# Last x tiles of the output product, step order of the second norm, and three first splits in one decoder layer

## The chip, the cores and the metric

The program runs on one core of one Trainium2 chip. The metric is the device time of one execution in microseconds (us), the median of the runs. The engines are TensorE (PE, matmuls, with its weight loads PEld), VectorE (DVE), ScalarE (ACT), GpSimd (POOL) and SyncE (SP), which here issues most DMAs. Each engine works through its own instructions in their order and waits on semaphores for the others.

## What is computed

One decoder layer on x (2048 rows, width 1024), all in 32-bit floats:

```
h    = RMSNorm(x) * (1 + scale1) + shift1
p    = h @ W_in            -> q, k, v (8 heads of 64), forget logits, x_in, B, C (512 each)
attn = causal softmax(q.k/8 + F[t] - F[s]) v,   F = cumsum(log sigmoid(...)), q and k normed by head
conv = B * dwconv3(C * x_in)
x1   = x + gate1 * (concat(attn, conv) @ W_out)
h2   = RMSNorm(x1) * (1 + scale2) + shift2
u    = dwconv3(h2 @ W_up)             (2 x 2816 columns)
out  = x1 + gate2 * ((silu(u_gate) * u_val) @ W_down)
```

## The kernel before

A 32-bit product is made as three matmuls on split operands (`mm3`, L142): high by high, high by low, low by high. ACT makes the high part of a tile, and DVE then the low part as the difference, so each new operand costs one step on ACT and, behind it, one on DVE. What is wrapped in `K(...)` keeps its place in the program's order on its engine; the rest is placed by the scheduler that builds the program, by its own estimate.

**Columns of W_in.** `project` (L484) makes k and then q: it first loads and splits its eight slices of weights (`w_slice` L167, high L178, low L179), then goes through 16 tiles of 128 rows; after a tile's matmuls come the steps of the norm by head (square on ACT, sums and a Newton root on 8 columns on DVE, L517 to L521). Then the loop at L652 makes x, c and b, column group by column group, from slices that it loads and splits at its start. DVE also works on other things in that stretch, such as `mo` (L546, L548), the modulation vector's products.

**Attention, and the start of the output product.** Attention runs in steps of one block of 128 queries of two heads. A block's `nb` (L895) and two exponentials (L898) on ACT follow the maxima on DVE (L881); PE transposes the first nine 128-column blocks (`near`, L918, copied by L920 and L925), a transposing DMA the others (`far`, L911); then come the products with the values (L954 to L956) and the division (L962). Step 64 is behind the last scores; what it still runs is the end of steps 62 and 63. There the generator `mixed` is started.

**The output product.** `mixed` (L788) goes through 64 units n: quarter Q of the rows (4 tiles of 128), half hf of the columns (512), and i, one of the eight parts of the inner length. `prepare` (L775) makes a unit's operands: for Q = 0 the pair `wp` of the weights, and for hf = 0 the pair `mp` of the mixed tile `src` (L771 high, L772 low), written into the buffer that held a weight tile `wo`. It runs up to three units ahead. Unit i = 6 has no matmuls, unit i = 7 has those of both, 24; every other unit has 12 (three for each of the four row tiles), of 128x128 by 128x512. At i = 2 of hf = 0 the four x tiles of the quarter are loaded (L801), for Q = 1 into wide tiles, else into four `raw` tiles of 128x1024, of which there are four in all (`raw_tile`, L710). At i = 7 DVE adds x (L812), which also frees the accumulators for the next half, and for hf = 1 the sums are stored through POOL's queue (L814).

**The second norm, beside it.** From unit 17 on, one step of `norm2` runs after each unit: for a quarter the squares (L1093), the root and the scaling (L1100), and then by column blocks. `columns` transposes a block on PE (L1068) and copies it with scale and shift on ACT (L1070); one accumulator buffer serves all these transposes. `operand` splits a block (L1058 high, L1059 low). An even Q has two blocks (b11, b21) by k; an odd Q has b1 and b2 by k and forms the sums of a seven-product scheme: t1, t2, t3, t4 (`diff` L1061, `last_operands` L1073), in five steps per k, each splitting as it goes.

**The up weights.** `up_weights(i)` (L1142) loads two raw tiles (L1146), scales them on ACT (L1152) and forms seven pairs. The first pair has tiles of its own; from i = 1 on they are `raw` tiles. In `up` the first product of an i is copied on ACT (`p1`, L1271) before the same accumulator is used on (L1226). The weights of i + 1 are begun ahead of that copy in the program's order.

## Time and profile before

| | |
|---|---|
| median of 3 runs | 2475.0 us (2469.92 to 2476.56) |
| the profiled execution | 2468.95 us, its span 2467.1 us |
| PE busy | 2364.3 us (96%) |
| DVE, ACT, POOL busy | 1790.0, 1256.6, 358.6 us |
| DMA | 368.70 MB, mean 149 GB/s |

The stages in the span: first norm and v up to 160 us, k and q to about 357, x, c, b to 632, attention to 970, output product to 1165, then up and down for the first half of the rows to 1825 and for the second to the end. In a timeline a row is the start, the length, engine, line and operation, `out<-in`, partitions and shape, the number of like instructions in a row, and in brackets the idle time just ahead of the row and what ended it. The clock is the share of TensorE's full speed that was granted.

### The profile page before, as it was taken

The page shows a single profiled execution, that of the slowest core. Times are in us where ns is not written, and L with a number is a line of the kernel's source. Part 1 is how long each engine was busy: PE and PEld are TensorE (multiplying, and loading weights), DVE is VectorE, ACT ScalarE, POOL GpSimd, SP SyncE. Part 2 cuts the span into 40 slices and gives each one's busy share as a digit, 9 for nine tenths or more (in the row PEclk, how much of TensorE's full clock was granted, in tenths as well). Part 3 has the DMA queues.
Part 4 walks back from the last instruction along what each step waited for, and adds up shares of the span by engine and source line. Part 5 has one row for each costly group of instructions (what it writes and reads, how often), then busy time and mean ns, then how long its engine had stood idle before and what let it go on. Part 6 is the DMA issues. An engine that isn't in the chain of part 4 may idle for free.

```text
span 2467.1 us, 38327 instructions
## 1 busy us (share of the span) xinstructions
PE 2364.3 (96%) x14419; PEld 1585.8 (64%) x14419; DVE 1790.0 (73%) x3333; ACT 1256.6 (51%) x2016; POOL 358.6 (15%) x298
## 2 busy tenths in 40 slices
PE   4999999999899888998999999999999999999999
PEld 4988788888677666444444444688764444448887
DVE  7566784452799887456788888767778888885554
ACT  3533443221588887333556556555455655554333
POOL 4210111011577785000000000000000000000000
PEclk9999999999999999999999999999999999999999
DMA  8334686443598987523322222677652222226775
GB/s 240 147 118 128 169 234 194 147 147 95 119 187 178 204 170 156 181 103 127 95 86 86 87 84 77 197 225 244 205 162 86 86 90 82 94 88 219 229 228 184
DMA packets 428066, 368.70 MB, mean 149 GB/s; under 512 B 184080, under 2 KB 327784, under 8 KB 426856
## 3 DMA queue, kind: packets, MB, share of 16 engines
q1 hardware_dynamic: 420824, 349.40, 50.3%
q10 hardware_dynamic: 4752, 8.46, 1.0%
q0 software_dynamic: 2304, 8.39, 0.9%
q8 instruction: 113, 1.85, 0.3%
q14 instruction: 73, 0.60, 0.1%
HBM read 267.54 MB, written 65.08 MB: 135 GB/s over the span
## 4 chain that ended last, share of the span: by engine, by line
PE 77%; DVE 7%; DMA 6%; issue 5%; ACT 3%; POOL 1%; SPq 1%; ACTq 0%; DVEq 0%; POOLq 0%
PE acc L1226 32%; PE acc L142 24%; PE pr L142 10%; PE pv L142 3%; DMA far<-wide 3%; PE pt L918 1%; PE ps L857 1%; PE ps L858 1%; DVE near L925 1%; PE po L954 1%; DVE s_t L881 1%; DMA wx<-in_w_up_dram 1%; PE po L956 1%; PE po L955 1%; ACT s_t L898 1%
## 5 line engine op out<-in xcount | busy, mean ns | idle before, releaser
L1226 PEld LDWEIGHTS <-pair 128*128 128x128 f16 x3696 | 362.0, 98 | 443.2 <-issue 8.4
L1226 PE MATMUL acc<-t,pair 128*128 128x512 f16 x2112 | 477.4, 379 | 0.0
L1226 PE MATMUL acc<-b,pair 128*128 128x512 f16 x1584 | 364.9, 380 | 5.9 <-ACT t L1271 5.9
L1198 DVE TENSOR_TENSOR lo<-raw,hi 128x1024 fp32r<-128x1024 f32 x176 | 211.7, 1223 | 141.9 <-ACT hi L1197 141.1
L142 PE MATMUL acc<-hi 128*128 128x512 f32 x704 | 276.9, 393 | 3.4 <-DVE t L1049 3.4
L142 PE MATMUL acc<-lo,hi 128*128 128x512 f32 x704 | 274.3, 390 | 0.3 <-DVE lo L1198 0.3
L142 PE MATMUL acc<-hi,lo 128*128 128x512 f32 x704 | 274.2, 389 | 0.0
L1197 ACT ACTIVATE hi<-raw 128x1024 fp32r<-128x1024 f32 x176 | 181.8, 1054 | 163.8 <-PE acc L142 131.1
L1239 DVE SCALAR_TENSOR_TENSOR w<-w,fcw,w 128x1024 f32<-128x1024 f32 x176 | 226.1, 1285 | 34.6 <-ACT w L1234 25.3
L142 PE MATMUL acc<-wp,mp 128*128 128x512 f16 x768 | 172.2, 383 | 6.9 <-DVE raw L812 4.1
L1130 ACT ACTIVATE pair<-raw 128x1024 f16<-128x1024 f32 x132 | 138.2, 1049 | 69.1 <-DVE raw L1127 69.1
L898 ACT ACTIVATE s_t<-s_t,nb,cst 128x2048 f32<-128x2048 f32 (+15 forms) x128 | 164.7, 1288 | 5.2 <-ACT nb L895 0.4
L1234 ACT ACTIVATE w<-w,fcw 128x1024 f32<-128x1024 f32 x88 | 100.7, 1144 | 130.6 <-DVE w L1126 130.6
L1133 DVE TENSOR_TENSOR pair<-raw,pair 128x1024 f16<-128x1024 f32 x132 | 160.8, 1219 | 6.8 <-ACT pair L1130 6.8
L592 ACT ACTIVATE wx<-wx 128x512 f32<-128x512 f32 x88 | 55.6, 632 | 202.5 <-DMA wx<-in_w_up_dram 167.6
L142 PEld LDWEIGHTS acc<-hi 128*128 128x128 f32 x704 | 132.1, 188 | 34.1 <-DVE t L1049 5.5
L142 PE MATMUL pr<-hh,wh 128*128 128x512 f32 x384 | 153.4, 399 | 0.2 <-ACT wh L178 0.2
L142 PE MATMUL pr<-hh,wl 128*128 128x512 f32 x384 | 150.9, 393 | 1.1 <-DVE wl L179 1.1
L142 PE MATMUL pr<-hl,wh 128*128 128x512 f32 x384 | 151.0, 393 | 0.0
L142 PEld LDWEIGHTS acc<-hi,lo 128*128 128x128 f32 x704 | 132.2, 188 | 27.7
L142 PEld LDWEIGHTS acc<-lo,hi 128*128 128x128 f32 x704 | 132.2, 188 | 27.4 <-DVE lo L1198 0.7
L910 POOL TENSOR_TENSOR wide<-s_t,wide 128x1024 f16<-128x1024 f32 x64 | 136.8, 2138 | 5.3
(296 smaller groups left out, 4714.6 us busy)
## 6 DMA issues: line engine op xcount, KB each, us to landing
raw<-in_w_up_dram SPq DMA_DIRECT2D x88, 512.0 KB, 3.7
raw<-y_sc SPq DMA_DIRECT2D x176, 256.0 KB, 3.7
raw<-in_w_down_dram SPq DMA_DIRECT2D x176, 256.0 KB, 4.1
wx<-in_w_up_dram SPq DMA_DIRECT2D x88, 256.0 KB, 2.9
y_sc<-w SPq DMA_DIRECT2D x44, 512.0 KB, 2.6
wm<-in_w_ada_dram SPq DMA_DIRECT2D x128, 128.0 KB, 3.0
wr<-in_w_in_dram SPq DMA_DIRECT2D x40, 256.0 KB, 3.5
x_t<-in_x_dram SPq DMA_DIRECT2D x16, 512.0 KB, 5.3
```

The lines of the kernel that those rows point to most:

```text
L142: ins = T.matmul(acc, lhsT=a, rhs=b, start=st, stop=sp)
L592: K(A.activation(t, t, AF.Abs, accum_out=l1[:, n : n + 1]))
L857: K(T.matmul(ps[:, 0:cw], lhsT=qt, rhs=kh[:, c0 : c0 + cw], start=True, stop=False))
L898: K(A.activation(cols, cols, AF.Exp, bias=nb[:, p : p + 1], scale=qk[:, 4:5], accum_out=un["l"][:, p : p + 1]))
L910: K(G.tensor_tensor(wide[:, 1, :], s_t[:, WB * P : WU], wide[:, 0, :], op=ALU.subtract))
L1130: K(A.activation(hi, raw, AF.Copy))
L1133: K(V.tensor_tensor(lo, raw, hi, op=ALU.subtract))
L1197: K(A.activation(hi, raw, AF.Copy))
L1198: K(V.tensor_tensor(lo, raw, hi.bitcast(F32), op=ALU.subtract))
L1226: K(T.matmul(acc, lhsT=a, rhs=b, start=st, stop=sp, skip_group_check=True))
L1234: K(A.activation(y, u[:, 0:1024], AF.Copy, scale=fcw[:, ct : ct + 1]))
L1239: K(V.scalar_tensor_tensor(y, u[:, m : m + 1024], fcw[:, m * 44 + ct : m * 44 + ct + 1], y, op0=ALU.mult, op1=ALU.add))
```

## The change

- `project` gets its slices and calls `following()` behind the matmuls of its last tile: k emits q's slices there, q emits x's first ones, ahead of the last tile's norm steps.
- `mixed` prepares unit 0 when it is started, and it is started before the work of step 64 is emitted. From unit 14 on it prepares five units ahead.
- The x of the last quarter is loaded by halves into 128x512 tiles that use the `src` buffers, 8 loads and 8 stores of half the size in place of 4 and 4.
- `norm2` for an odd Q takes four steps per k, in an order written for two engines, with two differences for t4 in place of three, and its last low part goes into the next step. The chain starts its second part after one empty step in place of four, and no step is taken behind a unit with i = 7.

```
+        def columns_of(col):
+            return [w_slice(w_in[k * P : (k + 1) * P, col : col + AW], [P, AW]) for k in range(KD)]
+        def project(w, col, gain, dst_hi, dst_lo, hooks, lull, following):
...
+                if i == NT - 1:
+                    after = following()
...
+        last_k, w_q = project(columns_of(AW), AW, ..., lambda: columns_of(0))
+        last_q, w_x = project(w_q, 0, ..., lambda: conv_slices(0, "x", 3 * AW + H))
...
+                w[name] = conv_slices(j, name, col) if j or name != "x" else w_x
...
     def mixed():
         todo = [(Q, hf, i) for Q in range(4) for hf in range(2) for i in range(8)]
-        ready = 0
+        prepare(*todo[0])
+        ready = 1
+        yield
         for n, (Q, hf, i) in enumerate(todo):
-            while ready < min(n + 3, 64):
+            while ready < min(n + (3 if n < 14 else 5), 64):
...
+            if Q == 3 and i == 2:
+                kept[3] = [fb.tile([P, 512], F32, tag=f"src{4 * hf + t}", name="x_q") for t in range(4)]
+                for xp, r in zip(kept[3], rows):
+                    K(nc.sync.dma_start(xp, x[r, n0 : n0 + 512]))
...
-                    if hf:
+                    if Q == 3:
+                        G.dma_start(x1_sc[Q * 4 + t][:, n0 : n0 + 512], xp)
+                    elif hf:
                         G.dma_start(x1_sc[Q * 4 + t], kept[Q][t])
...
+            if s == H * nu:
+                mix = mixed()
+                next(mix)
             n = 0
             while run or n < 3:
...
                 load_mixed(0, 7)
-                mix = mixed()
...
-        def last_operands(Q, k):
-            b21, t2 = bt["b21", k], bt["t2", k]
-            t4 = temp()
-            diff(t4, b21[0], t2[0])
-            diff(t4, t4, t2[1])
-            K(V.tensor_tensor(t4, t4, b21[1], op=ALU.add))
-            operand("t4", k, t4)
...
                 b1 = columns(Q, k)
+                if k:
+                    low(t4, *t4s)
                 yield
-                b2, t3 = columns(Q, 4 + k), temp()
-                operand("b22", k, b2)
+                b2, t3, t4 = columns(Q, 4 + k), temp(), temp()
+                b22, t1s, t2s, t3s, t4s = [pair(name, k) for name in ("b22", "t1", "t2", "t3", "t4")]
+                b11, b21 = bt["b11", k], bt["b21", k]
+                high(b2, b22[0])
                 diff(t3, b2, b1)
+                diff(b1, b1, b11[0])
+                low(b2, *b22)
                 yield
-                for e in bt["b11", k]:
-                    diff(b1, b1, e)
-                operand("t1", k, b1)
+                diff(b1, b1, b11[1])
+                high(b1, t1s[0])
+                high(t3, t3s[0])
+                diff(b2, b2, b1)
+                low(b1, *t1s)
+                low(t3, *t3s)
+                high(b2, t2s[0])
                 yield
-                diff(b2, b2, b1)
-                operand("t2", k, b2)
-                operand("t3", k, t3)
+                diff(t4, b21[1], b2)
+                low(b2, *t2s)
+                K(V.tensor_tensor(t4, t4, b21[0], op=ALU.add))
+                high(t4, t4s[0])
                 yield
-                last_operands(Q, k)
+            if Q % 2:
+                low(t4, *t4s)
                 yield
...
-        early = chain(steps[0], (None for _ in range(4)), steps[1], weights)
+        early = chain(steps[0], (None for _ in range(1)), steps[1], weights)
         for n, _ in enumerate(mix, 8):
-            if n >= 17:
+            if n >= 17 and n % 8 != 7:
                 next(early, None)
```

Line numbers move with it: the pairs of `prepare` are made at L778 and L779, x is added at L826, `high` and `low` are L1074 and L1077, `diff` is L1084, the copy of `columns` L1093, the up weights' load and scaling L1170 and L1176, the copy `p1` L1295. Three places show what moves.

ACT at step 64, before: `nb` and the exponentials (L898) of step 63, the copies L920 and L971 of the blocks' transposes, and the first pairs of the output product.

```order
L895 ACTIVATE nb<-mx,cst 128x2
L898 ACTIVATE s_t,l<-s_t,nb,cst 128x1152
L898 ACTIVATE s_t,l<-s_t,nb,cst 128x1024
L920 ACTIVATE near<-pt 128x512
L971 ACTIVATE tm<-pt,vi 128x512
L920 ACTIVATE near<-pt 128x512
L920 ACTIVATE near<-pt 128x128
L771 ACTIVATE wp<-wo,rim 128x512
L771 ACTIVATE mp<-src,rim 128x512
```

And now:

```order
L778 ACTIVATE wp<-wo,rim 128x512
L778 ACTIVATE mp<-src,rim 128x512
L911 ACTIVATE nb<-mx,cst 128x2
L914 ACTIVATE s_t,l<-s_t,nb,cst 128x1152
L914 ACTIVATE s_t,l<-s_t,nb,cst 128x1024
L936 ACTIVATE near<-pt 128x512
L987 ACTIVATE tm<-pt,vi 128x512
L936 ACTIVATE near<-pt 128x512
L936 ACTIVATE near<-pt 128x128
```

The first pair moved from the end of the row to its head.

DVE around unit 39, the end of the third quarter's first half, before: the last two scalings of the norm, a mixed tile's low part, the low part of b22, t3, and then the four sums that free the accumulators.

```order
L1100 TENSOR_SCALAR w_13811<-w_13811,ss 128x1024
L1100 TENSOR_SCALAR w_13812<-w_13812,ss 128x1024
L772 SCALAR_TENSOR_TENSOR mp<-src,rim,mp 128x512
L1059 TENSOR_TENSOR b_14288<-t_14285,b_14288 128x512
L1061 TENSOR_TENSOR t_14287<-t_14285,t_14278 128x512
L812 SCALAR_TENSOR_TENSOR raw<-acc,rim,raw 128x512 x4
L1061 TENSOR_TENSOR t_14278<-t_14278,b_13911 128x512 x2
```

And now:

```order
L1115 TENSOR_SCALAR w_13822<-w_13822,ss 128x1024
L1084 TENSOR_TENSOR t_14287<-t_14285,t_14266 128x512
L1084 TENSOR_TENSOR t_14266<-t_14266,b_13911 128x512
L1077 TENSOR_TENSOR b_14289<-t_14285,b_14289 128x512
L1084 TENSOR_TENSOR t_14266<-t_14266,b_13911 128x512
L1084 TENSOR_TENSOR t_14285<-t_14285,t_14266 128x512
L1077 TENSOR_TENSOR t_14290<-t_14266,t_14290 128x512
L1077 TENSOR_TENSOR t_14292<-t_14287,t_14292 128x512
L826 SCALAR_TENSOR_TENSOR raw<-acc,rim,raw 128x512 x4
```

The third and fourth differences and two more low parts stand ahead of the sums now; t3 and the low part of b22 have changed places.

SP at the end of the output product, before: the loads of mixed tiles (`src`), of the third and the last quarter's x, and of the up weights from i = 1 on.

```order
L801 DMA raw<-in_x_dram 128x1024 x4
L766 DMA src<-m_at_72 128x512
L766 DMA src<-m_at_73 128x512
L766 DMA src<-m_at_74 128x512
L801 DMA raw<-in_x_dram 128x1024 x4
L1146 DMA raw<-in_w_up_dram 128x8x128 x8
```

And now:

```order
L811 DMA raw<-in_x_dram 128x1024 x4
L773 DMA src<-m_at_74 128x512
L815 DMA x_q<-in_x_dram 128x512 x5
L1170 DMA raw<-in_w_up_dram 128x8x128 x2
L815 DMA x_q<-in_x_dram 128x512
L1170 DMA raw<-in_w_up_dram 128x8x128 x2
L815 DMA x_q<-in_x_dram 128x512 x2
L1170 DMA raw<-in_w_up_dram 128x8x128 x4
```

The last quarter's x no longer goes through `raw`, and the first up weights stand between its half tiles.

## Rows read from the trace of the kernel before

**Rows 1.** the span by windows: start:end, length, busy us (instructions) by engine, clock, DMA share, GB/s

```profile
955.00:1000.00 45.00, 36.87 (x411) 24.30 (x410) 27.63 (x61) 26.01 (x45) 9.22 (x6) 0.89 0.65 165
1000.00:1165.00 165.00, 158.37 (x756) 75.17 (x755) 95.25 (x160) 61.74 (x96) 8.21 (x15) 0.99 0.34 119
1180.00:1572.00 392.00, 392.00 (x1818) 178.28 (x1817) 345.03 (x384) 232.80 (x343) 0.00 (x0) 1.00 0.28 89
```

**Rows 2.** TensorE's timeline, start of x: start, length, operation, [idle before <- its releaser]

```profile
359.08 0.50 PE L142 MATMUL pr<-hh,wl 128*128 128x512 f32 x1 [1.11 <-DVE wl L179]
```

**Rows 3.** TensorE's timeline, end of attention and first products of the output

```profile
967.36 1.09 PE L918 MATMUL pt<-ident,s_t 128*128 128x128 f32 x4
...
973.88 4.31 PE L142 MATMUL acc<-wp,mp 128*128 128x512 f16 x12 [2.69 <-ACT mp L771]
...
981.03 2.75 PE L142 MATMUL acc<-wp,mp 128*128 128x512 f16 x12
```

**Rows 4.** TensorE's timeline, third and last quarter of the output product

```profile
1086.98 0.66 PE L1068 MATMUL pt<-ident,w 128*128 128x128 f32 x4 [0.87 <-ACT t L1070]
...
1117.78 4.03 PE L142 MATMUL acc<-wp,mp 128*128 128x512 f16 x12 [2.94 <-DVE raw L812]
...
1136.41 0.66 PE L1068 MATMUL pt<-ident,w 128*128 128x128 f32 x4 [0.78 <-ACT t L1070]
...
1143.43 6.88 PE L142 MATMUL acc<-wp,mp 128*128 128x512 f16 x31 [1.18 <-DVE raw L812]
```

**Rows 5.** timelines of ScalarE and of TensorE at the start of the up stage

```profile
1172.69 2.19 ACT L1152 ACTIVATE raw<-raw,cst 128x1024 f32<-128x1024 f32 x2 [14.12 <-DMA raw<-in_w_up_dram]
1174.79 0.57 ACT L1271 ACTIVATE t<-acc 128x512 f32<-128x512 f32 x1
...
1175.41 4.22 PE L1226 MATMUL acc<-b,pair 128*128 128x512 f16 x12 [5.89 <-ACT t L1271]
```

**Rows 6.** windows as in group 1, right behind the three longest of these waits

```profile
973.80:978.10 4.30, 4.22 (x15) 1.55 (x16) 2.83 (x4) 2.56 (x5) 0.00 (x0) 0.62 1.07 223
...
1117.70:1121.80 4.10, 4.02 (x14) 1.67 (x14) 2.66 (x5) 0.00 (x0) 2.12 (x4) 0.67 0.65 261
...
1175.40:1179.70 4.30, 4.29 (x14) 1.66 (x14) 1.97 (x3) 0.17 (x3) 0.00 (x0) 0.65 0.33 100
```

**Rows 7.** VectorE's timeline, last tile of q, first slice of x

```profile
357.87 0.48 DVE L548 SCALAR_TENSOR_TENSOR mo<-wm,cact,mo 128x256 f32<-128x256 f32 x1
...
358.34 0.69 DVE L179 TENSOR_TENSOR wl<-wr,wh 128x512 fp32r<-128x512 f32 x1
```

**Rows 8.** VectorE's timeline around step 64

```profile
963.17 0.17 DVE L758 TENSOR_SCALAR rim<-rim 128x2 f32<-128x2 f32 x1
...
965.98 0.28 DVE L925 TENSOR_TENSOR near<-pt,near 128x128 f16<-128x128 f32 x1
```

**Rows 9.** ScalarE's timeline around step 64

```profile
964.70 0.30 ACT L895 ACTIVATE nb<-mx,cst 128x2 f32<-128x2 f32 x1 [2.64 <-DVE mx L881]
965.09 1.35 ACT L898 ACTIVATE s_t<-s_t,nb,cst 128x1152 f32<-128x1152 f32 x1
...
973.10 0.72 ACT L771 ACTIVATE mp<-src,rim 128x512 f16<-128x512 f32 x1 [0.82 <-DVE wp L772]
```

**Rows 10.** SyncE's queue: a transposing DMA, and the loads of the last quarter's x

```profile
971.25 1.95 SPq L911 DMA_TRANSPOSE far<-wide  x1
...
1120.95 6.19 SPq L801 DMA_DIRECT2D raw<-in_x_dram  x4
```

**Rows 11.** waits from 1000 to 1165: waiter <- releaser: us in all, times, longest

```profile
DVE t L1059 <- ACT t L1058: 8.4, 12, 0.7
```

**Rows 12.** timelines of VectorE and ScalarE, the norm's steps in that stretch

```profile
1104.09 0.78 ACT L1070 ACTIVATE t<-pt,sh,a 128x512 f32<-128x512 f32 x1 [1.79 <-PE pt L1068]
...
1093.52 1.41 DVE L1061 TENSOR_TENSOR t<-t,b 128x512 f32<-128x512 f32 x2
...
1115.70 0.69 DVE L1059 TENSOR_TENSOR t<-t,t 128x512 f16<-128x512 f32 x1 [0.69 <-ACT t L1058]
```

More of the change, by code (lines that the diff above doesn't have):

```diff
@@ L481, in value_tiles @@
                 splits.append(value_tile(i))
-        def project(col, gain, dst_hi, dst_lo, hooks, lull):
-            w = [w_slice(w_in[k * P : (k + 1) * P, col : col + AW], [P, AW]) for k in range(KD)]
+        def columns_of(col):
+            return [w_slice(w_in[k * P : (k + 1) * P, col : col + AW], [P, AW]) for k in range(KD)]
+        def project(w, col, gain, dst_hi, dst_lo, hooks, lull, following):
             def finish(i, qn):
@@ L533, in finish_last, with conv_slices @@
                     value_tiles(NT)
-            return finish_last
+            return finish_last, after
+        def conv_slices(j, name, col):
+            return [
+                w_slice(
+                    w_in[hf * 512 : (hf + 1) * 512, col + j * P : col + (j + 1) * P].rearrange("(k p) n -> p k n", p=P),
+                    [P, 4, P],
+                )
+                for hf in range(2)
+            ]
         def modulate(m):
@@ L629, in up_scales @@
             yield
-        last_k = project(AW, gq[:, 1:2], k_hi, k_lo, {0: largest_gains, 1: gain_scales, 3: running_sum, 5: running_offset, 7: largest_value, 9: value_scale}, (0, 13))
-        last_q = project(0, gq[:, 0:1], q_hi, q_lo, {0: last_k, 1: last_k, 3: piece, 6: piece, 9: piece, 12: piece, 15: piece}, (2, 15))
+        last_k, w_q = project(columns_of(AW), AW, gq[:, 1:2], k_hi, k_lo, {0: largest_gains, 1: gain_scales, 3: running_sum, 5: running_offset, 7: largest_value, 9: value_scale}, (0, 13), lambda: columns_of(0))
+        last_q, w_x = project(w_q, 0, gq[:, 0:1], q_hi, q_lo, {0: last_k, 1: last_k, 3: piece, 6: piece, 9: piece, 12: piece, 15: piece}, (2, 15), lambda: conv_slices(0, "x", 3 * AW + H))
         def load_head(h):
@@ L654 @@
             for name, col in (("x", 3 * AW + H), ("c", 3 * AW + H + 2 * CD), ("b", 3 * AW + H + CD)):
-                w[name] = [
-                    w_slice(
-                        w_in[hf * 512 : (hf + 1) * 512, col + j * P : col + (j + 1) * P].rearrange("(k p) n -> p k n", p=P),
-                        [P, 4, P],
-                    )
-                    for hf in range(2)
-                ]
+                w[name] = conv_slices(j, name, col) if j or name != "x" else w_x
             zp = None
@@ L798, in mixed @@
             if hf == 0 and i == 2:
-                kept[Q] = [wide_temp()[:, 0:D] if Q == 1 else raw_tile() for _ in range(4)]
-                for xp, r in zip(kept[Q], rows):
-                    K(nc.sync.dma_start(xp, x[r, :]))
+                if Q < 3:
+                    kept[Q] = [wide_temp()[:, 0:D] if Q == 1 else raw_tile() for _ in range(4)]
+                    for xp, r in zip(kept[Q], rows):
+                        K(nc.sync.dma_start(xp, x[r, :]))
+            if Q == 3 and i == 2:
+                kept[3] = [fb.tile([P, 512], F32, tag=f"src{4 * hf + t}", name="x_q") for t in range(4)]
+                for xp, r in zip(kept[3], rows):
+                    K(nc.sync.dma_start(xp, x[r, n0 : n0 + 512]))
             if i == 0:
@@ L1053, with high, low, pair @@
         bt = {}
-        def operand(name, k, raw):
+        def high(raw, hi):
+            K(A.activation(hi, raw, AF.Copy))
+        def low(raw, hi, lo):
+            K(V.tensor_tensor(lo, raw, hi, op=ALU.subtract))
+        def pair(name, k):
             both = fp.tile([P, 1024], F16, tag=f"{name}{k}", name=name)
-            bt[name, k] = hi, lo = both[:, 0:512], both[:, 512:1024]
-            K(A.activation(hi, raw, AF.Copy))
-            K(V.tensor_tensor(lo, raw, hi, op=ALU.subtract))
+            bt[name, k] = both[:, 0:512], both[:, 512:1024]
+            return bt[name, k]
         diff = lambda o, a, b: K(V.tensor_tensor(o, a, b, op=ALU.subtract))
@@ L1105, in norm2 @@
                     for n, name in enumerate(("b11", "b21")):
-                        operand(name, k, columns(Q, 4 * n + k))
+                        h = columns(Q, 4 * n + k)
+                        hi, lo = pair(name, k)
+                        high(h, hi)
+                        low(h, hi, lo)
                         yield
@@ L1127 @@
         sub = lambda o, a, b: K(V.tensor_tensor(o, a, b, op=ALU.subtract))
-        def high(raw, hi):
-            K(A.activation(hi, raw, AF.Copy))
-        def low(raw, hi, lo):
-            K(V.tensor_tensor(lo, raw, hi, op=ALU.subtract))
         used = [0]
```

2 lines of the change are left out of this document (1 added, 1 removed).

## The prediction

> **What bounds the kernel now.** I read the busy time by stage first, then the matmul engine's own timeline with what ended each of its idle times, then the other engines' timelines at those places. TensorE (PE) works through nearly all of every stage, so a change gains only where PE stands idle or runs at its lower clock, and the question at each place is which engine's result ended the wait. By stage [rows 1], PE stands still for 45.00 − 36.87 = 8.13 us around the end of attention and the start of the output product (955 to 1000), for 165.00 − 158.37 = 6.63 us in the rest of that product (1000 to 1165), and for nothing in the 392 us that follow 1180. That last row decides how a gain counts: once the up stage has begun, PE has no hole in which an early start could be lost, so what is won before 1180 reaches the end whole, unless a later wait grows.
>
> The waits that the edits aim at are these. At the start of the x columns PE waits 1.11 us for VectorE's (DVE's) low split of the first slice [rows 2]. At the start of the output product it waits 2.69 us for ScalarE's (ACT's) high part of the first mixed tile, and the 12 matmuls after it take 4.31 us where the next 12 take 2.75 [rows 3]. Inside the product there are four more waits, 0.87, 2.94, 0.78 and 1.18 us [rows 4]. At the start of the up stage it waits 5.89 us for an ACT copy, which itself stands behind two ACT scalings that had waited 14.12 us for a weight load [rows 5]. The granted clock is 0.62, 0.67 and 0.65 in the three stretches after the waits of 2.69, 2.94 and 5.89 us [rows 6], between the two levels of 1.2 and 2.4 GHz, so a part of each ran at the lower one. The waits of 0.87, 0.78 and 1.18 are followed by matmuls at full length [rows 4]. So a long wait is paid twice: 4.31 − 2.75 = 1.56, 4.03 − 2.75 = 1.28 and 4.22 − 2.75 = 1.47 us on top.
>
> **First splits moved up.** From k to q only three steps on 8 columns move behind the splits on DVE, and ACT's order there, which the high parts follow, is unchanged: 0, at most 0.5. From q to x, DVE's low split of the first slice moves ahead of a 0.48 us `mo` step and a small one; by the starts of the rows (357.87 to 358.34) that is 0.47 us sooner [rows 7]. The work ahead of it now still ends at 357.87, so of the 1.11 us 0.64 stays. The second slice of b is loaded earlier too; I give it 0.1. Together **0.6** (0 to 1.1, the whole wait).
>
> **Start of the output product (step 64).** Before, the pair for unit 0 (`wp`, `mp`) came last on ACT, behind the exponentials of step 63 and step 62's copies. Now it comes ahead of them. The scale is ready at 963.17 + 0.17 [rows 8], so `wp` high can run by 964.1. `mp` high must wait until DVE has made `wp` low, as the row at 973.10 does (0.82 behind it) [rows 9], because `mp` is written where the source of `wp` lies. On DVE `wp` low now stands behind the `near` step at 965.98 [rows 8], so it runs from 966.2 to 966.9, `mp` high to 967.7, `mp` low to 968.4. The price: `nb` of step 63 and its two exponentials wait behind `mp` on ACT, 967.7 instead of 964.70, 3.0 us [rows 9], and behind them wait PE's transposes for that step. PE had slack there: its transposes begin at 967.36, 0.9 us after the first exponential ended (965.09 + 1.35), and each later wait for them on ACT absorbs some. I follow the chain to about 1.4 us of delay at the last transposes: these end near 972.6 instead of 971.2 (973.88 − 2.69), and with `mp` ready the product starts at 972.6, 1.3 us earlier, after no long idle. The clock's 1.56 should come back in the main, though a new hole of 1 to 2 us ahead of the transposes may keep a part; I take 1.0 of it. Gain **2.3**; 0 if the 3.0 us pass through whole, 2.9 if the clock comes back whole. The cover that hides the rest: step 63's transposing DMA is issued at 971.25 [rows 10] and will be at 974.2; its product is wanted after 983. If that DMA took over 9 us, it would be late.
>
> **Inside the product.** Gone by the new order: the adjacent transposes at 1086.98 (0.87), the wait ahead of unit 48 (2.94, and 1.28 of clock), 0.78 and 1.18 [rows 4], 7.05 us in all. Why they go: per column block DVE made 12 subtractions and stood three times for 0.70 us while ACT made a high part (12 times, 8.4 us, for the four blocks) [rows 11]; now it makes 11 and has other work there. That shortens the chain of a block, which took from 1104.09 to 1116.4, by 3 × 0.70 + 0.69 = 2.8 us [rows 11, 12], and no step is put right ahead of the sums that free the accumulators. What comes new: at unit 39, seven DVE steps of the first block now stand ahead of the first sum, where two stood. Seven at 0.60 to 0.70 us [rows 12] after a copy that ends some 1.5 us after the transposes began (0.66 and 0.78) put the sum's start at 5.9 and its end at 6.6, while PE's own 24 matmuls, twice 2.75 us, end at 5.6: a wait of 1.0. And the transposes of blocks b1 and b2 of the third column now stand side by side at units 45 and 46, with a high part of the block before and an `mp` ahead of the copy on ACT: nearest is 0.78, which has that pattern [rows 4]; worked through the queue I get 2.2. At 3.2 us of new waits and 0.3 for a chance of lower clock, the gain is **3.5** (1.2 to 5.0: 7.05 less twice 2.94, the longest wait here, or less 1.18 and 0.87).
>
> **Start of the up stage.** The raw tiles of the second pair of up weights were held by the last quarter's x until its sums were stored. Now the x comes in half tiles on `src` buffers, and the four raw tiles come free with the third quarter's stores: the row shows them taken again from 1120.95 on [rows 10], 45 us ahead of the use. Eight loads of half the size in place of four, and eight stores in place of four, lie on queues with that slack. With the weights there, ACT's two scalings (2.19 us) run while the first product is still going, and the copy follows its product directly. Gone: 5.89 + 1.47 = **7.4** (6.4 if a wait of the 1 us kind stays). After that the next limit is the product itself.
>
> **Down stages.** The same steps of norm run there beside a PE with little idle; fewer DVE steps, one shift: 0 (1 worse to 1.5 better, of the size of the short waits read above).
>
> The sum is 0.6 + 2.3 + 3.5 + 7.4 = 13.8. The profiled execution took 2468.95 us, of which 2467.1 are its span; it lies 6 us under the median of 2475.0, and the fastest run shown is 2469.92. Against the profile the sum gives 2455; I carry it over to the median: 2475.0 − 13.8 = **2461**. About 0.3%, 7.4 us, is what a measurement of this kernel can tell from no change.
>
> A rule that speaks against a part of it: the clock terms. The rows show the lower clock directly behind waits of 2.69 and 2.94 us and not behind those of 1.18 and less. The Trainium skill, "TensorE: Matmul & The Clock Gate", section "HAM oscillation — how this bites in real kernels", lets the clock fall only behind idle gaps longer than these two; by it they cost no clock, 1.0 + 1.28 would not come back, and the sum would be 11.5. The trace does not bear this out, so it has a small chance, in the first rival.
>
> **Rivals.** (1) The slow stretches have another cause than the wait in front of them and stay in number, moved: the sum loses 1.0 + 1.28, and 1.47: 13.8 − 3.7 = 10.1, 2465. For it: nothing in the rows shows why; against it: all three follow the three longest waits. (2) ACT's strict order eats the gains of the output product: the 3.0 us pass through at step 64, and in the loop the two new waits are long enough to bring the clock down, 2 × (2.9 + 1.3) = 8.4 against 7.05. Then only 7.4 and some of 0.6 stay: about 2468. For it speaks that high parts and `mp` stand ahead of the copies that PE waits for. (3) The change doesn't do what it says for the raw tiles: the weight loads stand behind x loads on SP's queue, and if these wait for `src` buffers until late, the up stage waits as before: 13.8 − 7.4 = 6.4, 2469. Against it: the `src` tiles are read out by `mp` well before unit 55. (4) Slower: the norm chain falls behind. A block now has four units of about 3.1 us (2.75 and a part of the transposes), 12.4 us, where it had five. If its chain did not shrink but grew, ACT and DVE would lag at each of the three boundaries behind units 39, 47 and 55 and again ahead of the up stage's operands. It turns the sign when a block takes over 12.4 + 13.8 / 3 = 17 us; at 18, 3 × 5.6 − 13.8 = 3.0 gives 2478. The chain read above is 12.2 us before the cut, so I see little for it.
>
> **How the numbers follow.** Forecast 0.72 (its own range 2457 to 2468, from the low and the high ends of the terms), rival 1 0.06, rival 2 0.11, rival 3 0.07, rival 4 0.04. The range from 2453 to 2470 takes in the terms' bounds, a few us of scatter of a median of this kernel, and rivals 1 to 3. Faster by over 0.3% means under 2467.6: the forecast but for its edge (0.70), rival 1, half of rival 2 and a quarter of rival 3 make 0.83; same 0.13; slower, rival 4, 0.04.
>
> **What the profile after would show.** Right: no wait over 1 us at the first up products and 12 of them in 2.75; the start of the output product near 972.6 at a full clock, with step 63's exponentials 3 us later; new waits of 1 and 2 us at units 40 and 46 and none ahead of unit 48; about 0.6 us at x. Wrong: an idle of 3 us ahead of step 63's transposes, a clock near 0.65 in a new place, a weight load still ending a wait near 1165, or holes after 1180 that were not there.

## The result, and where the time went

The changed kernel takes 2455.2 us (median of 4 runs, 2452.39 to 2458.83) where the kernel before takes 2474.8 on the same chip: a ratio of 0.9923, with an interval of 0.9903 to 0.9942. Two later comparisons, each with its own runs of the kernel before, give 0.9927 [0.9914, 0.9939] and 0.9920 [0.9907, 0.9932]. That is 18 to 20 us; the forecast was 2461, a gain of 13.8, in a range of 2453 to 2470. By profile the gain is 16.6 us (2468.95 to 2452.39), the span going from 2467.1 to 2450.4.

The span is cut at starts of rows on TensorE: the first product of the x columns, the first scores of attention, the first product behind the wait for the last division (4.37 us in these two profiles, so it is a good mark), the 12 products of unit 1, the first product of up, and of down. For the changed kernel these stretches read (start:end, length, busy us and instructions of PE, PEld, DVE, ACT, POOL, then clock, DMA share, GB/s):

```profile
355.01:628.87 273.86, 273.11 (x1198) 222.14 (x1198) 121.32 (x249) 63.31 (x145) 34.31 (x36) 1.00 0.48 141
628.87:963.74 334.87, 297.50 (x4437) 228.57 (x4438) 300.70 (x969) 277.37 (x546) 246.37 (x156) 0.99 0.90 179
963.74:976.39 12.65, 11.14 (x141) 9.31 (x141) 7.32 (x14) 9.27 (x17) 3.18 (x2) 0.82 0.47 110
976.39:1156.97 180.58, 176.50 (x932) 85.58 (x931) 101.13 (x172) 73.94 (x114) 9.88 (x19) 0.99 0.44 149
1156.97:1555.64 398.67, 398.67 (x1850) 180.75 (x1848) 347.31 (x388) 233.17 (x346) 1.03 (x2) 1.00 0.28 90
1555.64:1807.26 251.62, 249.52 (x1122) 203.80 (x1120) 173.82 (x214) 131.16 (x156) 0.00 (x0) 1.00 0.70 229
```

Cut at the same places, the two kernels compare so:

| stretch | before | changed | gain | forecast |
|---|---|---|---|---|
| start to x | 357.26 | 355.01 | 2.25 | 0 |
| x, c, b columns | 275.94 | 273.86 | 2.08 | 0.6 |
| attention | 332.91 | 334.87 | −1.96 | 0 |
| last division to unit 1 | 14.92 | 12.65 | 2.27 | 2.3 |
| unit 1 to up | 183.15 | 180.58 | 2.57 | 3.5 |
| first up | 406.19 | 398.67 | 7.52 | 7.4 |
| first down | 253.92 | 251.62 | 2.30 | 0 |
| second up and down | 642.81 | 643.14 | −0.33 | 0 |
| span | 2467.1 | 2450.4 | 16.7 | 13.8 |

TensorE's timeline of the changed kernel, which answers to [rows 2 to 5] (start, length, operation, and in brackets the idle time ahead and who ended it):

```profile
355.01 0.48 PE L142 MATMUL pr<-hh,wh 128*128 128x512 f32 x1
...
355.56 0.40 PE L142 MATMUL pr<-hh,wl 128*128 128x512 f32 x1
...
963.74 0.21 PE L970 MATMUL po<-v,near 128*128 128x64 f16 x1 [4.37 <-DVE at L978]
964.99 1.10 PE L934 MATMUL pt<-ident,s_t 128*128 128x128 f32 x4
969.61 2.75 PE L142 MATMUL acc<-wp,mp 128*128 128x512 f16 x12
976.22 0.33 PE L934 MATMUL pt<-ident,s_t 128*128 128x128 f32 x1 [1.00 <-ACT tm L987]
976.39 2.75 PE L142 MATMUL acc<-wp,mp 128*128 128x512 f16 x12
...
1036.32 0.66 PE L1091 MATMUL pt<-ident,raw 128*128 128x128 f32 x4 [0.87 <-ACT t L1093]
...
1088.08 5.37 PE L142 MATMUL acc<-wp,mp 128*128 128x512 f16 x24 [1.00 <-DVE raw L826]
...
1107.29 0.66 PE L1091 MATMUL pt<-ident,w 128*128 128x128 f32 x4 [2.17 <-ACT t L1093]
...
1156.97 2.75 PE L1250 MATMUL acc<-b,pair 128*128 128x512 f16 x12
```

The wait at x is gone, and so are those of 2.69, 2.94 and 5.89 us with the slow matmuls behind them. The forecast's two new waits, 1.0 and 2.2, stand there as 1.00 and 2.17, and a new slow stretch stands behind the second (shown below, with the terms). The wait of 0.87 at 1036.32 is not new: the forecast counts four waits in the product before, but there were five, and this one was the first of them and stayed:

```profile
1040.95 0.66 PE L1068 MATMUL pt<-ident,raw 128*128 128x128 f32 x4 [0.87 <-ACT t L1070]
```

At step 64, ACT's order and its price can be read directly, to hold against [rows 9]:

```profile
962.33 0.72 ACT L778 ACTIVATE wp<-wo,rim 128x512 f16<-128x512 f32 x1 [2.64 <-DVE mx L897]
964.58 0.72 ACT L778 ACTIVATE mp<-src,rim 128x512 f16<-128x512 f32 x1 [1.53 <-DVE wp L779]
965.21 0.28 ACT L911 ACTIVATE nb<-mx,cst 128x2 f32<-128x2 f32 x1
```

`nb` comes 1.47 us after the mark, where it came 1.41 ahead of it: 2.88 us later (3.0 forecast). And SP's queue and ACT at the up stage, to hold against [rows 5, 10]:

```profile
1116.71 2.55 SPq L1170 DMA_DIRECT2D raw<-in_w_up_dram  x2
```

```profile
1143.27 2.17 ACT L1176 ACTIVATE raw<-raw,cst 128x1024 f32<-128x1024 f32 x2
1159.76 0.60 ACT L1295 ACTIVATE t<-acc 128x512 f32<-128x512 f32 x1 [14.31 <-PE acc L1250]
```

The weights of the second pair are asked for at 1116.71, the scalings are done 14 us ahead of the copy, and the copy now waits for PE instead of PE for it.

### The profile page after: what moved, and what is told of

Read it like the earlier page. It is cut to its first block, busy times and chain, and to the rows that moved or that the text cites. A ratio compares the mean times of both kernels' runs of the same rounds, so it can differ in the third digit from the quotient of the medians.

```text
span 2450.4 us, 38339 instructions
## 1 busy us (share of the span) xinstructions
PE 2361.1 (96%) x14419; PEld 1586.0 (65%) x14419; DVE 1782.4 (73%) x3325; ACT 1257.3 (51%) x2016; POOL 361.3 (15%) x302
## 4 chain that ended last, share of the span: by engine, by line
PE 79%; DVE 7%; issue 5%; DMA 4%; ACT 3%; POOL 2%; SPq 1%; ACTq 0%; DVEq 0%; POOLq 0%
PE acc L1250 33%; PE acc L142 26%; PE pr L142 11%; PE pv L142 2%; DMA far<-wide 2%; PE pt L934 1%; DVE near L941 1%; PE ps L873 1%; DVE s_t L897 1%; PE ps L874 1%; PE po L970 1%; DVE acc L235 1%; PE po L972 1%; PE po L971 1%; POOL wide L926 1%
## 5 line engine op out<-in xcount | busy, mean ns | idle before, releaser
L1074 ACT ACTIVATE pair<-raw 128x1024 f16<-128x1024 f32 x132 | 138.3, 1048 | 68.5 <-DVE raw L1157 68.5
L1077 DVE TENSOR_TENSOR pair<-raw,pair 128x1024 f16<-128x1024 f32 x132 | 160.9, 1219 | 4.7 <-ACT pair L1074 4.7
```

The lines of the kernel that those rows point to most:

```text
L1074: K(A.activation(hi, raw, AF.Copy))
L1077: K(V.tensor_tensor(lo, raw, hi, op=ALU.subtract))
```

## The experiments

Twelve kernels were run, each with its profile, the changed kernel three times. The stretches of all of them, in us:

| kernel | attention | division to unit 1 | unit 1 to up | first up | first down | median |
|---|---|---|---|---|---|---|
| before | 332.91 | 14.92 | 183.15 | 406.19 | 253.92 | 2474.8 |
| changed, and again twice | 334.87, 335.74, 334.70 | 12.65, 12.64, 12.64 | 180.58, 180.57, 180.58 | 398.67 | 251.62, 251.67, 251.70 | 2455.2, 2454.31, 2455.22 |
| undo_xq | 337.80 | 12.64 | 178.88 | 406.82 | 251.63 | 2464.91 |
| undo_norm | 336.84 | 12.64 | 184.15 | 398.67 | 253.90 | 2462.96 |
| undo_start | 336.17 | 14.83 | 178.89 | 398.67 | 251.61 | 2456.55 |
| undo_split | 338.67 | 12.64 | 180.57 | 398.68 | 251.62 | 2457.65 |
| undo_norm3 | 335.31 | 12.64 | 180.58 | 398.67 | 253.89 | 2459.78 |
| xq_alone | 338.81 | 15.33 | 183.22 | 398.67 | 253.91 | 2468.06 |
| old_places | 337.96 | 12.64 | 180.77 | 398.68 | 251.60 | 2457.38 |
| shift_steps | 339.63 | 12.64 | 180.31 | 398.67 | 251.71 | 2457.43 |
| late_mp | 336.09 | 11.22 | 180.33 | 398.67 | 251.69 | 2452.38 |
| late_mp_skip45 | 336.45 | 11.48 | 177.36 | 398.67 | 251.70 | 2450.43 |

The medians are from several sets of runs; the kernel before took 2474.8 us in that of the result, and in the others 2472.03 (undo_xq to undo_split), 2472.46 (the changed kernel's second, shift_steps, late_mp, undo_norm3) and 2475.21 (its third, late_mp_skip45, xq_alone, old_places). The preparation five units ahead was not undone by itself: every kernel but the one before and xq_alone has it.

**The raw tiles.** First the changed kernel with the x of the last quarter in raw tiles again:

```
-                if Q < 3:
-                    kept[Q] = [...]
-            if Q == 3 and i == 2:
-                kept[3] = [fb.tile([P, 512], F32, tag=f"src{4 * hf + t}", name="x_q") for t in range(4)]
...
+                kept[Q] = [wide_temp()[:, 0:D] if Q == 1 else raw_tile() for _ in range(4)]
...
```

> The changed kernel with the last quarter's x again in raw tiles (four loads of 128x1024, four stores). Theory: the 7.5 us that the start of the up stage gained come from the raw tiles alone. Then the first up products wait again 5.5 to 6.5 us for the copy behind the up weights, the next 12 products take about 4.2 us, nothing else moves, and the time is 7 to 8 us above the changed kernel's, about 2463 against 2455. Rival: the order of the norm's steps brought the weights' own steps forward and did part of it; then less than 5 us come back.

Its time is 2464.91 us (ratio to before 0.9968 [0.9955, 0.9980]), 9.7 above the changed kernel's where 7 to 8 were expected. PE and ACT at the start of its up stage:

```profile
1171.57 4.80 PE L1243 MATMUL acc<-b,pair 128*128 128x512 f16 x12 [5.94 <-ACT t L1288]
...
1168.86 2.19 ACT L1169 ACTIVATE raw<-raw,cst 128x1024 f32<-128x1024 f32 x2 [22.17 <-DMA raw<-in_w_up_dram]
```

The wait and the slow products are back, 406.82 − 398.67 = 8.15 us. The other way round, the kernel before with the half tiles alone:

> The kernel before with the last quarter's x in half tiles and nothing else. Theory: the up stage starts 7.5 to 8 us sooner (398.7 us from its first product to the down stage in place of 406.2) and nothing else moves: x with a first wait near 1.1, 14.9 us from the last division to unit 1, the product at 183.2, the first down stage at 253.9. Attention took 332.9 us in the kernel before and 334.9 to 339.6 in nine kernels that have parts of the change: if it is again near 333, something in the change costs 2 us or more there; if it is above 334.5, that was scatter.

It runs at 0.9976 [0.9963, 0.9989] of the kernel before, 7.2 us by the medians, its up stage takes 398.67, and its later stages stay what they were. The term is shown from both sides.

**Step 64.** The changed kernel with the product begun as before:

```
-        prepare(*todo[0])
-        ready = 1
-        yield
+        ready = 0
...
-            if s == H * nu:
-                mix = mixed()
-                next(mix)
...
+                mix = mixed()
```

> The changed kernel with the output product begun as before: no pair prepared ahead of step 63's exponentials. Theory: PE waits 2.7 us again ahead of the first product and the 12 products after it take 4.3 us, while step 63's exponentials start 3 us sooner; from the wait for the last division (4.4 us) to unit 1's products it takes 2.3 us more, and the time is 2.3 us above the changed kernel's. Rival: the gain there belongs to where the lower clock happens to fall; then the products' start moves by under 1 us.

The stretch takes 14.83 us, 2.2 more, and the wait and the slow clock return:

```profile
973.54 4.28 PE L142 MATMUL acc<-wp,mp 128*128 128x512 f16 x12 [2.69 <-ACT mp L778]
980.66 2.75 PE L142 MATMUL acc<-wp,mp 128*128 128x512 f16 x12
```

Its median, 2456.55, is only about 1 to 2 us above the changed kernel's, where 2.3 were expected. In the profile 1.7 of the 2.2 us come back in the product, which has no lower clock there (below); whether this kernel's other runs had none either is not recorded.

**The norm's steps.** The changed kernel with the old steps and their old places, in both quarters that have them, and then with the old steps for the last quarter alone:

> The changed kernel with the old steps of the norm, five per column block, and their old places (from unit 17, four empty steps). Theory: the output product's waits were set by the order of those steps. Then the waits of 0.87 between adjacent transposes, near 2.9 ahead of unit 48 with a slow clock behind it, and 0.8 and 1.2 come back, the new ones of 1.00 and 2.17 go, and the product from unit 1 to the up stage takes 2.6 us more (the stage's change as measured). The down stage of the first half gained 2.3 us that I had not forecast: if the norm's order did that, its waits of 0.3 to 1.2 us at accumulators near the end come back and it takes 2 us more; if it was the landing of loads, it does not, or by chance. In all 2.6 to 5 us above the changed kernel, 2458 to 2460.

> The changed kernel with the old five steps per block for the last quarter's norm alone, which runs beside the first down stage. Theory: the 2.28 us that the first down stage won come from the new steps. Then it takes 253.9 us in place of 251.6, all else as in the changed kernel. Rival: they come from the loads that the earlier parts shifted; then it stays at 251.6.

With all of them undone the product takes 184.15 us, and two of its waits are the old ones (0.87 ahead of the transposes and 1.18 ahead of unit 56), the one ahead of unit 48 is even longer, and that of 0.78 is not there:

```profile
1088.53 0.66 PE L1091 MATMUL pt<-ident,w 128*128 128x128 f32 x4 [0.87 <-ACT t L1093]
...
1120.54 4.44 PE L142 MATMUL acc<-wp,mp 128*128 128x512 f16 x12 [4.14 <-DVE raw L826]
```

The median of undo_norm is 7.8 us above the changed kernel's, where 2.6 to 5 were expected. By the profile 3.6 are in the product and 2.3 in the first down stage; the rest lies ahead of them, where profiles scatter. The kernel before took 183.15 for the product with the same steps, so what they cost depends on the rest of the change too, and 3.6 is their price only in the changed kernel.

The first down stage takes 253.90 and 253.89 us with the old steps of the last quarter, in either kernel, 253.91 in xq_alone, and 251.6 to 251.7 in the ten profiles with the new ones. So the 2.3 us there are the steps' own. TensorE's waits in that stage, for undo_norm3 (who waited, for whom: us in all, times, longest):

```profile
PE acc L142 <- DVE t L1067: 3.5, 8, 1.2
PE acc L142 <- DVE lo L1281: 0.3, 1, 0.3
```

and for the changed kernel:

```profile
PE acc L142 <- DVE t L1067: 1.6, 5, 0.4
PE acc L142 <- DVE lo L1222: 0.5, 1, 0.5
```

The waiting products are the first of a row group; they need an accumulator that DVE frees with a product and a sum (L1067, L1068 here, L1049, L1050 before), which stand in DVE's order behind the norm's steps. Three fewer waits and a longest one of 0.4 instead of 1.2 us make 1.7 of the 2.3. For the other 0.6 PE was busy that much longer with the old steps (250.08 against 249.52 us), which was not traced further. The median of undo_norm3 is 5.5 us above the changed kernel's beside it, where 2.3 were expected; by the profiles the rest lies ahead of x, which begins at 359.00 against 354.56.

Is it the order within the steps or their places? The new steps in the old places:

```
-        early = chain(steps[0], (None for _ in range(1)), steps[1], weights)
+        early = chain(steps[0], (None for _ in range(4)), steps[1], weights)
...
-            if n >= 17 and n % 8 != 7:
+            if n >= 17:
```

> The changed kernel with the new steps of the norm, but from unit 17 on behind every unit, with four empty steps, as the old ones were placed. Theory: the order within the steps removed the waits ahead of units 48 and 56 (2.9, 1.2 and 0.8 us), the places decide only which transposes stand side by side. Then there are two waits of 0.87, one near 2.2 at units 45 and 46, none of 1 us or more ahead of units 48 and 56, and the product takes 179 to 181 us. Rival: the free unit at each end of a half did it; then 2 us or more come back ahead of unit 48.

The product takes 180.77 us, with waits of 0.87, 0.87 and 2.17 us and none ahead of units 48 and 56. The new steps removed those (their order, with one difference fewer; the two were not taken apart); the free unit at the end of a half did not.

**The first splits.** The changed kernel with q's and x's first slices behind the last tile's steps:

```
-                if i == NT - 1:
-                    after = following()
...
-            return finish_last, after
+            return finish_last, following()
```

> The changed kernel with q's and x's first slices emitted behind the last tile's norm steps, as before. Theory (order): the wait for the first low split of x is back at 0.5 to 1.1 us, the one at q's first high split stays what it is, and the stage is 0.5 to 1.2 us longer. Rival (landing): both first waits are set by an ACT step that stands ahead of the first high split and waits for a load of another weight; then both waits vary by about 1 us from run to run with that landing, whatever the order, and q's wait in this run and in the other three kernels of this call, which all have the early order, is spread over 0.5 to 1.7 us.

Its first wait in x is 1.38 us. Over all profiles, this wait is 1.11, 0.85 and 1.38 us in the three kernels with the late order (before, xq_alone, undo_split; mean 1.11), and between 0 and 1.46 us in the eleven profiles with the early one, five of them with none (mean 0.43). The stretch x to attention is 275.42 to 277.05 us with the late order and 273.86 to 275.56 with the early one. By these means, three profiles against eleven with overlapping ranges, the order is worth about 0.7 us and the landing of loads about as much. The 277.05 holds a lower clock besides: in undo_split the granted clock is 0.63 in the 4.6 us behind the wait of 1.38.

```profile
357.80:362.40 4.60, 4.52 (x13) 3.58 (x14) 4.53 (x16) 2.61 (x6) 0.62 (x1) 0.63 0.96 284
```

The wait at q's first high split is 1.64, 1.92 and 1.94 us with the late order (mean 1.83), and with the early one anything from 0.17 to 1.92 or no such wait (mean 0.99). Five of those eleven lie between 1.61 and 1.92, so the order alone does not remove it, as the rival had it; whether it makes it rarer is not shown. In the kernel before, ACT had waited 2.30 us for a load of another weight just ahead of that split; in the changed one the same step came 2.14 us sooner, though the work ahead of it on PE came only 1.09 us sooner:

```profile
253.34 0.63 ACT L592 ACTIVATE wx<-wx 128x512 f32<-128x512 f32 x1 [2.30 <-DMA wx<-in_w_up_dram]
```

```profile
251.20 0.63 ACT L605 ACTIVATE wx<-wx 128x512 f32<-128x512 f32 x1 [2.28 <-DMA wx<-in_w_up_dram]
```

**Beyond the change.** Three waits were left in the product, 0.87, 1.00 and 2.17 us. I tried to move them away by moving three steps by one unit:

```
-        early = chain(steps[0], (None for _ in range(1)), steps[1], weights)
+        early = chain(steps[0], steps[1], weights)
...
-            if n >= 17 and n % 8 != 7:
+            if n >= 17 and n % 8 != 7 and n not in (22, 38):
```

> The changed kernel with three of the norm's steps moved by one unit: the empty step goes, and no step is taken behind units 22 and 38. Theory: the three waits left in the product are set by where the steps fall (transposes side by side at units 21 and 22, a step too many ahead of unit 39's sums, transposes side by side at 45 and 46). Then 0.87, 1.00 and 2.17 us go, and with them the lower clock, and the product from unit 1 to the up stage takes 174.8 us in place of 180.6 or 178.9; the time is 4 to 6 us below the changed kernel's. Rival: the chain of steps is the limit by now, and the waits only move to units 48 or 56; then less than 2 us are won.

The rival held. The product takes 180.31 us: the transposes meet elsewhere, and the second column's late steps now end behind the products of unit 47:

```profile
1067.06 0.66 PE L1091 MATMUL pt<-ident,raw 128*128 128x128 f32 x4 [0.87 <-ACT t L1093]
...
1118.82 4.43 PE L142 MATMUL acc<-wp,mp 128*128 128x512 f16 x12 [2.30 <-DVE raw L826]
```

Upon the same placement, step 64 with `wp` ahead of the exponentials and `mp` behind them:

> As the kernel with the moved steps, and at step 64 only the weight pair of unit 0 stands ahead of step 63's exponentials; the pair of the mixed tile follows them. Theory: the 3 us that the exponentials were delayed for the pair were partly paid on TensorE (two waits of 0.5 and 1.0 us for a copy). Then the exponentials start 3 us sooner, the first product still does not wait, and from the last division to unit 1 it takes 11 to 12 us in place of 12.65. Rival: the exponentials' delay was hidden in full and the product's start now waits for the pair; then 12.6 or more.

The stretch to unit 1 takes 11.22 us, 1.4 less, as the theory had it; the exponentials' `nb` comes 0.8 us ahead of the mark in place of 1.5 behind it, 2.3 us sooner where 3 were expected. With this, and only the step behind unit 45 moved:

```
-            if n >= 17 and n % 8 != 7:
+            if n >= 17 and n % 8 != 7 and n != 45:
```

> The changed kernel with only the weight pair of unit 0 ahead of step 63's exponentials, as in the run before, and one step of the norm moved: none is taken behind unit 45, so that the transposes of the third column's two blocks no longer stand side by side, while the second column's steps stay where they are. Theory: from the last division to unit 1 11.2 us in place of 12.65, and the wait of 2.17 us goes without one in its place ahead of unit 48, since the steps whose sums are late there were not moved; the product takes 177 to 178.5 us in place of 180.6; the time is 2 to 5 us below the changed kernel's. Rival: the wait moves again, as with three steps moved; then only the 1.4 us are won.

> The changed kernel beside the others of this call, for their ratio. Its stages are as in the other two profiles from the last division on.

The kernel without a step behind unit 45 takes 2450.43 us (2448.05 to 2451.58) beside 2455.22 (2452.61 to 2457.38) for the changed kernel on the same chip, 0.9898 [0.9884, 0.9912] of the kernel before. The product takes 177.36 us, and its waits are:

```profile
1089.28 5.37 PE L142 MATMUL acc<-wp,mp 128*128 128x512 f16 x24 [1.00 <-DVE raw L831]
...
1125.56 0.66 PE L1098 MATMUL pt<-ident,w 128*128 128x128 f32 x4 [0.24 <-ACT t L1100]
...
1134.20 20.91 PE L142 MATMUL acc<-wp,mp 128*128 128x512 f16 x96 [0.21 <-DVE x_q L831]
```

(The wait of 0.87 at units 21 and 22 is there as well.) By its stretches it gains 1.2 and 3.2 us, 4.4 of the 4.8.

The changed kernel's second run was made for the spread of its stages:

> The changed kernel once more, beside the others of this call. Theory: its stages come out as before where the order sets them: 12.65 us from the last division to unit 1, 251.6 for the first down stage, 398.7 for each up stage; the output product at 180.6, or 178.9 if the wait of 2.17 us at units 45 and 46 brings no lower clock this time. The stages up to the last division vary by some us with the landing of loads. If attention is again above 334 us, where the kernel before took 332.9, the change or the place in time costs it; if it is below, it is scatter.

The stages that the order sets came out so (12.64, 180.57, 398.67 and 251.67 us), and attention was above 334 again, 335.74.

**Attention.** The profile of the kernel before has the shortest attention of all, 332.91 us. I had asked whether the change costs something there; xq_alone answers it: it has attention as in the kernel before, and takes 338.81. Among the other kernels it runs from 334.7 to 339.6. Block by block, the profiles agree to 0.1 us for the first third and part ways after, where PE waits for the transposing DMAs. In xq_alone, for one:

```profile
818.05 0.20 PE L961 MATMUL po<-v,far 128*128 128x64 f16 x1 [2.96 <-DMA far<-wide]
...
906.78 0.20 PE L961 MATMUL po<-v,far 128*128 128x64 f16 x1 [3.60 <-DMA far<-wide]
```

The waits are the smaller part, though. Here is all of attention in the kernel before, then in xq_alone, and the stretches behind the latter's two waits:

```profile
633.20:966.11 332.91, 295.41 (x4437) 227.51 (x4438) 300.77 (x969) 277.75 (x547) 246.33 (x156) 1.00 0.91 180
```

```profile
632.16:970.97 338.81, 300.06 (x4437) 229.72 (x4438) 300.41 (x969) 278.74 (x547) 246.68 (x156) 0.99 0.91 177
817.90:822.50 4.60, 4.41 (x37) 3.28 (x38) 0.70 (x2) 1.38 (x3) 4.18 (x3) 0.63 0.80 201
906.70:911.30 4.60, 4.41 (x37) 3.26 (x38) 0.77 (x2) 1.45 (x3) 4.22 (x4) 0.63 0.31 70
```

Of the 5.9 us that xq_alone takes longer, PE's idle time makes 1.25 (38.75 against 37.50) and its busy time 4.65, with the same number of matmuls: much of it is the lower clock behind these two waits, about 1.7 us at each (an estimate: 4.60 us at 0.63). The kernel before has it behind none of its waits for these DMAs.

This does not answer why the three profiles of the changed kernel lie within 1.1 us of each other at the low end, while shift_steps, with the same program there, lies 4 us higher, which may also be why its median (2457.43) is higher than the changed kernel's (2454.31). What decides the landing of these DMAs stays open.

## Why the prediction was right, and which terms were off

**What bounds the kernel** was read rightly: a gain ahead of the up stage comes through whole, since once its weights are there the up stage has no idle time in any of the profiles and takes 398.67 us.

**Up stage, 7.4**: 7.5 in the profile, 8.15 and 7.5 us when undone or done alone. The two parts of the sum, wait and slow products, are both there. The rival that the loads stay late, so that the change doesn't free the tiles, fell. So did the first rival here and at step 64: undone, the slow products came back together with their wait (4.80 us behind 5.94, 4.28 behind 2.69).

**Step 64, 2.3**: 2.27, but the shares were others. The product began 5.87 us after the mark where I had worked out 6.5 (7.77 before), so 1.9 and not 1.3 was won there; the clock came back whole, 2.75 us in place of 4.31, where I took 1.0 of 1.56; and 1.2 were lost again behind the first product, at PE's wait of 1.00 for a copy that the delayed exponentials had pushed back, which I had not followed so far. That loss is the price of `mp` ahead of the exponentials, and late_mp took it back.

**Product, 3.5**: 2.57. The forecast left out one of the five waits, which stayed, so the sum does not change. The places and the sizes of the waits that come and go were right, the lower clock was not: I gave it 0.3 of a us behind the wait of 2.17. A part of the second rival came true: of the two new waits, one was long enough to bring the clock down. Behind the other, of 1.00, the products are at full length (5.37 us for 24). The granted clock of the stretch behind the wait of 2.17, in the changed kernel, and in undo_start, which has the same wait:

```profile
1107.40:1112.00 4.60, 4.60 (x16) 1.99 (x17) 4.41 (x7) 3.09 (x5) 0.00 (x0) 0.63 0.38 114
```

```profile
1111.60:1116.20 4.60, 4.60 (x24) 2.35 (x25) 4.40 (x8) 3.15 (x5) 0.00 (x0) 1.00 0.38 114
```

Of eight profiles with that wait, six have the low clock and 180.57 to 180.77 us for the product; two have none and 178.88 and 178.89. It costs 1.7 us (180.58 − 178.88); without it the product gains 4.3, more than forecast and inside the term's bounds. The Trainium skill, "TensorE: Matmul & The Clock Gate", section "HAM oscillation — how this bites in real kernels", would have the clock stay up after so short a gap; six of these eight profiles do not agree.

**First splits, 0.6**: the order's share at x is about 0.7 by the means of fourteen profiles; the profile's 2.08 us hold the luck of a load beside it. The 2.25 us ahead of x are not shown to be a gain of the change: 1.09 were there before the first edited place (the last tile of k, 252.96 to 251.87), the rest is the load ahead of q's split, and over the profiles with the early order x begins anywhere from 353.66 to 359.00, with the late one from 355.80 to 357.26.

**First down stage, 0**: this is the step that failed. I wrote that the norm's steps run beside a PE with little idle, and looked at PE alone. What mattered was DVE's queue: the products and sums that free the accumulators stand behind those steps, so the new steps end PE waits. It is worth 2.3 us, beyond the term's bound of 1.5, and two thirds of what the same steps are worth in the product of the changed kernel (184.15 − 180.58). The rows for its longest wait stood in the trace of before: a low part of the norm had stood 0.70 us for its high part on ACT, then came a low part of the weights, then the step that PE waited for.

```profile
1758.56 0.69 DVE L1059 TENSOR_TENSOR t<-t,t 128x512 f16<-128x512 f32 x1 [0.70 <-ACT t L1058]
1760.66 0.68 DVE L1049 TENSOR_TENSOR t<-acc,gates 128x512 f32<-128x512 f32 x1
```

```profile
1761.49 0.47 PE L142 MATMUL acc<-hi 128*128 128x512 f32 x1 [1.16 <-DVE t L1049]
```

**From profile to median.** The median lies 2 us below the forecast's own range of 2457 to 2468 and inside the wider one, 2453 to 2470, which added scatter. I carried the sum of a profile, 2468.95, over to a median that was 6 us higher. The profile before has an attention about 6 us shorter than xq_alone's, so the profile understates the kernel before, and the median fell by 19.6 where the profile fell by 16.6. That the difference is attention's is argued from this, not shown. The terms' sum (13.8) is short of the profile by 2.9: 2.3 from the down stage; the 0.6 left is the net of the stretches ahead of x and in x (+2.25 and +1.5), attention (−2.0), the product (−0.9), the second half (−0.3) and small rests. That the product's shortfall is made up for by stretches that the change hardly touches is luck.

**The slower rival**, a norm chain that falls behind, did not happen in the changed kernel, but its mechanism is there: moved by one unit in shift_steps, the chain of the second column ends behind unit 47 and costs 2.30 us and the clock (12 products in 4.43 us). The forecast's chain of a block is 12.3 us by its rows, not 12.2; nothing hangs on that.

## What to carry to other kernels

Read a step's price on the queue that it stands in: an early operand pays for itself if what it is put ahead of has slack, and steps that run beside a busy engine are not free when they stand ahead of what frees its accumulators. Where a stage begins with a wait for a load, ask which tile holds its buffer, and whether that tile could lie elsewhere. And take the base of a forecast from several executions: a single profile of this kernel is uncertain by some 6 us in a stretch that the change doesn't touch.

## What was not expected of the hardware

The same wait of 2.17 us was followed by the lower clock in six executions and not in two. Its length does not decide elsewhere either. The forecast took from three places that the lower clock follows the long waits alone, but the trace of before has a wait of 3.35 us in attention with the clock at 1.00 behind it, and a stretch at 0.50 behind two waits of 1.64 and 1.09 at the start of q, one matmul apart:

```profile
255.20 0.49 PE L142 MATMUL acc<-wh,hh 128*128 128x512 f32 x1 [1.64 <-ACT wh L178]
256.79 0.79 PE L142 MATMUL acc<-wl,hh 128*128 128x512 f32 x1 [1.09 <-DVE wl L179]
...
903.58 0.20 PE L954 MATMUL po<-v,far 128*128 128x64 f16 x1 [3.35 <-DMA far<-wide]
```

```profile
257.00:260.00 3.00, 3.00 (x8) 2.32 (x9) 2.96 (x8) 0.77 (x2) 0.75 (x1) 0.50 0.92 224
903.50:908.10 4.60, 4.14 (x66) 3.34 (x67) 2.26 (x6) 2.96 (x7) 4.23 (x4) 1.00 0.36 81
```

What decides it stays open.

And one small step on DVE, two columns of integers, took 1.97 us in all fourteen profiles, where the same operation on the same tile, two steps ahead of it, takes 0.26 in the kernel before:

```profile
960.68 0.26 DVE L755 TENSOR_SCALAR rim<-rim 128x2 int32<-128x2 int32 x1
...
961.17 1.97 DVE L757 TENSOR_SCALAR rim<-rim 128x2 int32<-128x2 int32 x1
```

The last maxima stand behind it on DVE, and the wait of 4.37 us for the last division (4.88 in two profiles) ends after them. In the two profiles with 4.88 the first of the steps shown (L762 there) took 0.76 and 0.77 us in place of 0.25 to 0.27, which fits that a longer step here lengthens the wait by as much. I did not try to move or shorten these steps, so what could be won is open.
